# Probabilities times values in a forgetting-attention block: single key tiles against up to 512 query columns, nine full turned banks a head instead of ten partly filled ones

## The chip, the cores and the metric

The kernel runs on one core of one Trainium2 chip. The metric is the device time of one execution in microseconds (us). A core has five engines with instruction streams of their own: TensorE (PE, its weight loads shown apart as PEld), VectorE (DVE), ScalarE (ACT), GpSimd (POOL) and SyncE (SP, which here issues nearly all DMAs). Each stream runs in order, and the streams meet only where one instruction waits for another's semaphore.

## The reference, cut to what matters

The whole program is one decoder layer: RMSNorm, an input projection, forgetting attention beside chunked spatial gating, an output projection, and a convolutional gated MLP. The change lies in the attention alone. It has 1024 positions, 8 heads of 64, float32:

```python
logits = jnp.einsum('bqhd,bkhd->bhqk', qi, k).astype(jnp.float32) * scale
logits = logits + ci[..., None] - c_k                 # c: running sum of log-sigmoid forget gates
causal = pi[:, None] >= key_pos[None, :]
logits = jnp.where(causal, logits, -jnp.inf)
p = jax.nn.softmax(logits, axis=-1).astype(v.dtype)
return jnp.einsum('bhqk,bkhd->bqhd', p, v)
```

Queries are cut into 8 blocks of 128, here called rows j = 0 to 7, and keys into 8 tiles of 128, k = 0 to 7. The mask leaves the 36 blocks with k <= j.

## The kernel before, in words

**Number format.** TensorE works on float32r operands. To keep float32 accuracy a tensor is split into a rounded high part and the remainder, and products are summed over the parts. For the values, the high and the low part of V stand side by side as the 128 columns of one stationary operand, so one matmul gives both products, on partitions 0 to 63 and 64 to 127. The turned probabilities are split into high and low part too (s = 0, 1), so each product of a key tile with some query columns is two matmuls.

**A head, step by step.** The loop from line 1051 runs over 40 steps, five a head (s = 0 to 4), and works on two heads at once: the values of head h and the logits of head h+1. The order of TensorE's instructions is pinned by `seq`, which ties each to the one before. In each step TensorE gets, in this order:

1. the turns for the *next* step (`turn_p`, L946): blocks of probabilities, 128x128, are transposed into a PSUM bank. ScalarE casts the bank to the high part in a tile `pt` (L947), and VectorE subtracts to get the low part (L948). The tile pool gives `pt` three buffers.
2. for each group of this step: its value matmuls (`values`, L965), then the logits of the rows that `NEXT[s]` names (`logits_mm`, L906 and L907): rows 7, 6, then 5 and 4, then 3 and 2, then 1 and 0 in steps 0 to 4. VectorE takes from each row of logits the masked minimum of the negated logits (L919, `logits_min`).
3. in some steps (`FILLS`: steps 1 and 4 of heads 0 to 5, and three more of head 0's and the prologue's) a filler of 12 matmuls of the spatial gating's output projection (L990 to L992) with a VectorE add (L993).

The exponentials of the rows whose logits were made in a step are put on ScalarE at the end of the *next* step (`for e in last`, L1086 to L1088), behind that step's casts and, where there is one, behind its evacuation copy `out_copy` (L973). So rows 5 and 4 of head h+1 get their logits in step 2 and their exponentials (L929) in step 3; rows 3 and 2 in step 4; rows 1 and 0 in step 0 of the next head. In the last two heads the lists `held` and `last` shift this by a step.

**How the value product is tiled.** Queries go in pairs of rows: i = 3 is rows 6 and 7, i = 0 is rows 0 and 1. A group (h, i, k0) holds the two key tiles k0 and k0+1 against the 256 query columns of pair i: four blocks, or three where k0 = 2i lies on the diagonal. A head has ten groups: (3,0) (3,2) | (3,4) (3,6) | (2,0) (2,2) | (2,4) (1,0) | (1,2) (0,0), with | between steps. Six of their banks are 512 columns wide and four 384. Two PSUM banks a head, `po`, collect the result: rows 4 to 7, and rows 0 to 3. Each is evacuated by ScalarE and VectorE (L973, L974) into `attF`.

**Memory that is shared.** Four PSUM banks of tag `b` serve the turns, `po`, the filler and the turned row sums (`row_tail`, L868); two pairs of banks, tag `L`, serve the logits, so the logits of a row wait for the minimum of the row two before.

Of the kernel before, what the change touches and what calls it, by code (L numbers as in the profile page):

```python
# [12 lines left out]
ALU = mybir.AluOpType  # L13
AX = mybir.AxisListType
P = 128
# [44 lines left out]
def after(tc, later, earlier):  # L60
    tc.add_manual_dep(later.ins, earlier.ins.name, mybir.DependencyInfo(
        mybir.DependencyClass.NoSync, mybir.DependencyReason.DATA), reason="order")
# [3 lines left out]
def block_kernel(ctx: ExitStack, tc: tile.TileContext, xT, xtok, wuv, wv0, wv1, wqk, cpk, bfv,  # L66
                 ggain, g2r, gfr, wsp, woa, wos, wup, wdn, out):
    nc = tc.nc
    act, dve, pool, pe, sp = Line(nc.scalar, tc), Line(nc.vector, tc), Line(nc.gpsimd, tc), nc.tensor, nc.sync
# [13 lines left out]
    def nm(s):  # L83
        uid[0] += 1
        return f"{s}_{uid[0]}"
# [6 lines left out]
    def sb(tag, shape, dt=F32):  # L92
        return (raws if tag == "raw" else late if tag in LATE else early).tile(shape, dt, tag=tag, bufs=BUFS[tag], name=nm(tag))

    def bank():
        return psa.tile([P, 512], F32, tag="b", bufs=BB, name=nm("pb"))
# [7 lines left out]
    def f32(ap):  # L104
        return ap.bitcast(F32)
# [19 lines left out]
    ident = cst.tile([P, P], F32, name="ident")  # L125
# [77 lines left out]
    def psq(tag):  # L203
        return psa.tile([P, 512], F32, tag="s" if tag in "ab" else "b", bufs=4, name=nm("q" + tag))
# [12 lines left out]
    tj = sb("G", [P, 2, 2, 512])  # L217
# [478 lines left out]
    def seq(m):  # L696

        if order:
            after(tc, m, order[0])
        order[:] = [m]  # L700
# [106 lines left out]
    abs_, places = [None] * 8, {}  # L807
# [50 lines left out]
    attF = [None] * 4  # L858
# [15 lines left out]
    def pair_half(p, o):  # L874

        if attT[p] is None:
            attT[p] = sb("A" if p < 2 else "G", [P, 2, 1024], F32R)
        f, t = attF[p], attT[p]
        if p < 3:
            pool.tensor_tensor(out=f[:, 0, o], in0=f[:, 0, o], in1=f[:, 1, o], op=ALU.mult)  # L880
            pool.tensor_copy(t[:, 0, o], f[:, 0, o])
            pool.tensor_tensor(out=t[:, 1, o], in0=f[:, 0, o], in1=f32(t[:, 0, o]), op=ALU.subtract)
        else:
            dve.tensor_tensor(out=f[:, 0, o], in0=f[:, 0, o], in1=f[:, 1, o], op=ALU.mult)
            act.copy(t[:, 0, o], f[:, 0, o])
            dve.tensor_tensor(out=t[:, 1, o], in0=f[:, 0, o], in1=f32(t[:, 0, o]), op=ALU.subtract)
# [5 lines left out]
    def place():  # L892
        return psa.tile([P, 1024], F32, tag="L", bufs=2, name=nm("pl"))
# [4 lines left out]
    casts, los = [], []  # L898

    def logits_mm(h, j, ps):  # L900
        A, B, A2, B2 = abs_[h][:, 0, :], abs_[h][:, 1, :], a2s[0:66, h % 2, :], b2s[0:66, h % 2, :]
        n = (j + 1) * P
        qs = slice(j * P, (j + 1) * P)
        for c in range(0, n, 512):
            e = min(n, c + 512)
            seq(pe.matmul(ps[:, c:e], A[:, qs], B[:, c:e], start=True, stop=False))  # L906
            seq(pe.matmul(ps[:, c:e], A2[:, qs], B2[:, c:e], start=False, stop=True))  # L907
        return ps

    def logits_min(h, j, ps):  # L910

        i, jj = j // 2, j % 2
        w1, w2 = (2 * i + 1) * P, (2 * i + 2) * P
        if jj == 1:
            tp = sb(TTAG[i][h % 2], [P, w1 + w2])
            places[h, i] = (tp[:, 0:w1], tp[:, w1:w1 + w2])
        n = (j + 1) * P
        mn = sml.tile([P, 1], F32, tag="mn", name=nm("mn"))
        m = dve.tensor_tensor_reduce(out=places[h, i][jj], in0=ps[:, 0:n], in1=msk[:, 1024 - n:1024], scale=1.0,  # L919
                                     scalar=lim[:, 0:1], op0=ALU.add, op1=ALU.min, accum_out=mn)  # L920
        if h and j == 6:
            after(tc, m, recips[h - 1])
        if h and j == 3:
            after(tc, m, los[-1])
        return mn

    def logits_exp(h, j, mn):
        t = places[h, j // 2][j % 2]
        exs.append(act.activation(t, t, AF.Exp, bias=mn, scale=-1.0, accum_out=rows[h][:, j:j + 1]))  # L929
        return exs[-1]  # L930

    def logits(h, j):
        logits_exp(h, j, logits_min(h, j, logits_mm(h, j, place())))

    def turn_p(g):

        h, i, k0 = g
        tj = places[h, i]
        ptr = bank()
        pt = sb("pt", [P, 2, 512], F32R)  # L940
        diag = k0 == 2 * i
        blocks = [(k0, 0, 0), (k0, 1, 128)] + ([(k0 + 1, 1, 256)] if diag else
                                              [(k0 + 1, 0, 256), (k0 + 1, 1, 384)])
        w = 384 if diag else 512
        for k, jj, c in blocks:
            seq(pe.transpose(ptr[:, c:c + P], tj[jj][:, k * P:(k + 1) * P], ident))  # L946
        casts.append(act.copy(pt[:, 0, 0:w], ptr[:, 0:w]))  # L947
        los.append(dve.tensor_tensor(out=pt[:, 1, 0:w], in0=ptr[:, 0:w], in1=f32(pt[:, 0, 0:w]), op=ALU.subtract))  # L948
        return pt

    po = [None]

    def values(g, pt):
        h, i, k0 = g
        if i % 2 == 1 and k0 == 0:
            po[0] = bank()
        oc = (i % 2) * 256
        for s in range(2):
            for k in (k0, k0 + 1):
                lhs = V[k // 2][:, k % 2, h, :, :].rearrange("p s d -> p (s d)")  # L960
                half = k == 2 * i + 1
                o = (k - k0) * 256
                n = 128 if half else 256
                oo = oc + (128 if half else 0)
                seq(pe.matmul(po[0][:, oo:oo + n], lhs, pt[:, s, o:o + n], start=(k == 0 and s == 0),  # L965
                              stop=(s == 1 and half)))
        if i % 2 == 0 and k0 == 2 * i:
            p, hh = h // 2, h % 2
            o = slice((i // 2) * 512, (i // 2) * 512 + 512)
            r = slice(hh * 64, hh * 64 + 64)  # L970
            if attF[p] is None:
                attF[p] = sb("H", [P, 2, 1024])
            x = act.copy(attF[p][r, 0, o], po[0][64:128, :])  # L973
            dve.tensor_tensor(out=attF[p][r, 0, o], in0=po[0][0:64, :], in1=attF[p][r, 0, o], op=ALU.add)  # L974
            return x
        return None

    def sg_out(whs):
        for hf in range(2):
# [35 lines left out]
                pool.tensor_tensor(out=w[hf][:, 1], in0=src, in1=f32(w[hf][:, 0]), op=ALU.subtract)  # L1015
            wo.append(w)

    STEPS = [[(h, i, 2 * c) for i in (3, 2, 1, 0) for c in range(i + 1)] for h in range(8)]
    STEPS = [s[n:n + 2] for s in STEPS for n in range(0, 10, 2)]

    NEXT = (((7,), ()), ((6,), ()), ((5,), (4,)), ((3,), (2,)), ((1,), (0,)))

    def fill(key):
        for _ in range(FILL.get(key, 0)):
# [21 lines left out]
    for j in range(4, -1, -1):  # L1046
        logits(0, j)
        fill((-1, j))
    due = []
    turned = [turn_p(g) for g in STEPS[0]]  # L1050
    for n, step in enumerate(STEPS):
        h, s = n // 5, n % 5
# [7 lines left out]
        if h in (2, 4, 6) and s == 4:  # L1060
            for o in (slice(0, 512), slice(512, 1024)):
                pair_half(h // 2 - 1, o)
        now, turned = turned, [turn_p(g) for g in STEPS[n + 1]] if n + 1 < len(STEPS) else []
        last, due = due, []
        if n == 34:
# [10 lines left out]
        out_copy = None  # L1076
        for c, (g, pt, js) in enumerate(zip(step, now, NEXT[s])):
            out_copy = values(g, pt) or out_copy
            last_copy = out_copy
            if h < 7:  # L1080
                for j in js:
                    due.append((h + 1, j, logits_min(h + 1, j, logits_mm(h + 1, j, place()))))
            if s == (1 if h < 7 else 2) and c == (h == 7):
                row_tail(h)

        for e in last:  # L1086
            x = logits_exp(*e)
# [192 lines left out]
    for i in range(AHEAD):  # L1280
        for j in range(2):
            q = psq("a")
# [396 lines left out]
```

## Time and profile before

| | |
|---|---|
| median of 3 runs | 1058.69 us (1058.6 to 1058.9) |
| the profiled execution | 1059.72 us, its span 1058.0 us |
| instructions in the span | 14612 |
| TensorE busy | 1046.3 us, 99% of the span |
| VectorE, ScalarE, GpSimd busy | 884.0, 571.1, 235.8 us |
| first and last value matmul (L965) | 231.5 us, 370.0 us |

Rows of the profile give the engine, the line of the kernel, the operation, what it writes and reads, the shape, a count, and a duration; in the timeline the first column is the start in us from the span's start and the second the length of the run of like instructions. A matmul's length in a row includes its way through the array; the spacing of starts is what it costs in a stream. Where a row ends in brackets, they hold the idle time before it and what ended it. PEclk is the TensorE clock that was granted, in tenths of full speed.

### The profile page before, as it was taken

How to read it: one execution, taken by the hardware profiler on the slowest of the kernel's cores; microseconds unless marked ns; L12 is line 12 of the kernel's file. 1: busy time of each engine (PE TensorE's matmuls, PEld its weight loads, DVE VectorE, ACT ScalarE, POOL GpSimd, SP SyncE). 2: the span in 40 equal slices, each digit the busy share in tenths (PEclk: the TensorE clock that was granted, in tenths of full speed). 3: DMA queues.
4: the chain of work that ended last, by engine and by line, in shares of the span. 5: the costliest groups of instructions: out<-in, count | busy, mean ns of one | idle time of the engine just before them, and what ended most of it. 6: DMA issues, size and time to landing. Idle time of an engine off the chain costs nothing.

```text
span 1058.0 us, 14612 instructions
## 1 busy us (share of the span) xinstructions
PE 1046.3 (99%) x5156; PEld 880.3 (83%) x5156; DVE 884.0 (84%) x1297; ACT 571.1 (54%) x1013; POOL 235.8 (22%) x177
## 2 busy tenths in 40 slices
PE   9999999999999999999999999999999999999997
PEld 6988888988889888888888888888888888888885
DVE  6999787777778869998999989989897866897774
ACT  6776544456766746654444444444444544454653
POOL 0003241420420740154333323323321000000000
PEclk9999999999999999999999999999999999999999
DMA  9623466856555344222255322331322899333432
GB/s 323 219 8 134 129 162 167 224 153 190 168 163 170 122 174 173 72 89 100 80 170 179 120 96 94 120 122 59 132 96 80 302 328 314 102 99 100 146 119 94
DMA packets 67184, 155.78 MB, mean 147 GB/s; under 512 B 9028, under 2 KB 9748, under 8 KB 67112
## 3 DMA queue, kind: packets, MB, share of 16 engines
q1 hardware_dynamic: 65800, 154.82, 45.8%
q8 instruction: 40, 0.66, 0.3%
q14 instruction: 32, 0.26, 0.1%
q10 hardware_dynamic: 1312, 0.04, 0.1%
HBM read 111.96 MB, written 42.87 MB: 146 GB/s over the span
## 4 chain that ended last, share of the span: by engine, by line
PE 94%; DVE 2%; DMA 1%; ACT 1%; POOL 1%; issue 0%; SPq 0%; POOLq 0%; ACTq 0%; DVEq 0%
PE k L1529 20%; PE qc L1271 11%; PE qa L1271 11%; PE qd L1271 11%; PE ps L259 5%; PE qb L1271 5%; PE pb L259 5%; PE pb L965 3%; PE pb L946 3%; PE qa L417 2%; PE qc L417 2%; PE qd L417 2%; PE pl L906 2%; PE pl L907 2%; PE pf L990 1%; PE pf L992 1%
## 5 line engine op out<-in xcount | busy, mean ns | idle before, releaser
L1529 PE MATMUL k<-whb,wha 128*128 128x512 f32 x924 | 209.7, 389 | 0.0
L1529 PEld LDWEIGHTS k<-whb,wha 128*128 128x128 f32 x924 | 173.4, 188 | 36.2 <-DVE wha L161 0.2
L1271 PE MATMUL qc<-xT,whb 128*128 128x512 f32 x540 | 129.8, 389 | 0.2 <-ACT whb L155 0.2
L1271 PE MATMUL qa<-xB,wha 128*128 128x512 f32 x528 | 127.5, 390 | 0.0
L1271 PEld LDWEIGHTS qc<-xT,whb 128*128 128x128 f32 x540 | 101.3, 188 | 21.5 <-ACT whb L155 0.5
L1271 PEld LDWEIGHTS qa<-xB,wha 128*128 128x128 f32 x528 | 98.8, 188 | 20.9 <-DVE wha L161 0.4
L155 ACT CAST wha<-sg 128x512 fp32r<-128x512 f32 x77 | 47.8, 622 | 96.7 <-PE k L1529 86.4
L155 ACT CAST whb<-sg 128x512 fp32r<-128x512 f32 x82 | 50.5, 618 | 88.0 <-PE qc L1271 67.7
L161 DVE TENSOR_TENSOR wha<-sg,wha 128x512 fp32r<-128x512 f32 x77 | 52.7, 687 | 40.5 <-ACT wha L155 40.4
L947 ACT CAST pt<-pb 128x512 fp32r<-128x512 f32 (+1 forms) x80 | 42.2, 544 | 43.1 <-PE pb L946 34.2
L1271 PE MATMUL qd<-xB,whb 128*128 128x512 f32 x264 | 63.7, 389 | 0.0
L1271 PE MATMUL qd<-xT,whb 128*128 128x512 f32 x264 | 63.7, 389 | 0.0
L1155 POOL TENSOR_TENSOR sg<-raw 128x512 f32<-128x512 f32 x20 | 31.1, 1556 | 139.5 <-DVE whb L161 78.0
L1271 PE MATMUL qb<-xT,whb 128*128 128x512 f32 x252 | 61.0, 389 | 0.0
L161 DVE TENSOR_TENSOR whb<-sg,whb 128x512 fp32r<-128x512 f32 x82 | 57.0, 697 | 4.4 <-ACT whb L155 4.3
L948 DVE TENSOR_TENSOR pt<-pb,pt 128x512 fp32r<-128x512 f32 (+1 forms) x80 | 48.8, 634 | 12.3 <-ACT pt L947 11.0
L1271 PEld LDWEIGHTS qd<-xT,whb 128*128 128x128 f32 x264 | 49.5, 188 | 10.5 <-DVE u L1378 0.3
L1271 PEld LDWEIGHTS qd<-xB,whb 128*128 128x128 f32 x264 | 49.6, 188 | 10.3
L1271 PEld LDWEIGHTS qb<-xT,whb 128*128 128x128 f32 x252 | 47.2, 188 | 10.0 <-DVE whb L161 0.3
L965 PE MATMUL pb<-pt,V 128*128 128x256 f32 x320 | 52.1, 287 | 0.3 <-DVE pt L948 0.2
L1158 POOL TENSOR_TENSOR sg<-sg,raw 128x512 f32<-128x512 f32 x20 | 33.0, 1650 | 63.8 <-DVE whb L161 63.8
L965 PEld LDWEIGHTS pb<-pt,V 128*128 128x128 f32 x320 | 43.8, 190 | 2.6 <-DVE pt L948 0.4
(411 smaller groups left out, 2271.8 us busy)
## 6 DMA issues: line engine op xcount, KB each, us to landing
raw<-wup SPq DMA_DIRECT2D x44, 512.0 KB
sg<-hx SPq DMA_DIRECT2D x77, 256.0 KB
hx<-hs SPq DMA_DIRECT2D x44, 256.0 KB
hx<-ca SPq DMA_DIRECT2D x35, 256.0 KB
xT<-wdn SPq DMA_DIRECT2D x28, 256.0 KB
x<-kd SPq DMA_DIRECT2D x24, 256.0 KB
A<-xtok SPq DMA_DIRECT2D x8, 512.0 KB
raw<-wqk SPq DMA_DIRECT2D x8, 512.0 KB
```

Source lines behind the costliest of these rows:

```text
L155: act.copy(h, src)
L161: return eng.tensor_tensor(out=l, in0=src, in1=f32(h), op=ALU.subtract)
L259: pe.matmul(banks[m], xs(n, xi, k)[:, ms], w[:, wi, :], start=(first and k == 0 and c == 0 and (own or m % 2 == 0)), stop=(k == 3 and c == ...
L417: pe.matmul(ps, w[:, wi, ks], xs(n, xi, k), start=(first and c == 0), stop=(c == 11), skip_group_check=True)
L946: seq(pe.transpose(ptr[:, c:c + P], tj[jj][:, k * P:(k + 1) * P], ident))
L947: casts.append(act.copy(pt[:, 0, 0:w], ptr[:, 0:w]))
L948: los.append(dve.tensor_tensor(out=pt[:, 1, 0:w], in0=ptr[:, 0:w], in1=f32(pt[:, 0, 0:w]), op=ALU.subtract))
L965: seq(pe.matmul(po[0][:, oo:oo + n], lhs, pt[:, s, o:o + n], start=(k == 0 and s == 0), stop=(s == 1 and half)))
L1155: pool.tensor_tensor(out=s[0], in0=a21, in1=a22, op=ALU.add)
L1158: pool.tensor_tensor(out=s[3], in0=s[1], in1=a12, op=ALU.add)
L1271: pe.matmul(ps, w[:, wi, ks], xb[:, xi, k, :], start=(first and n == 0), stop=(n == 11), skip_group_check=True)
L1529: pe.matmul(banks[bk + m], xh[:, xi, ms], wh[:, wi, :], start=(first and p_ == 0 and n == 0), stop=(p_ == NP - 1 and n == 2), skip_group_c ...
```

## The change

The value product is cut the other way: one key tile k against all rows of a half that it reaches. Half 1 is rows 4 to 7, half 0 rows 0 to 3. A part (half, k) covers rows max(k, 4 half) to the end of the half, up to 512 columns. Parts are packed into nine groups of exactly four blocks: (1,0) to (1,4) alone, then (1,5) with (1,7), (1,6) with (0,2), (0,0) alone, and (0,1) with (0,3). The groups go two to a step, one in step 4, so the fifth entry of `NEXT` puts the logits of rows 1 and 0 behind that one group. The 36 turned blocks a head and the columns of the product are the same; the value matmuls are 24 a head instead of 40. Casts and subtractions are nine of 512 columns instead of six of 512 and four of 384. Both matmuls of one part now follow each other (s inside, k outside). The group (1,6)+(0,2) ends the first `po` bank and begins the second.

```diff
+    GROUPS = [((1, k),) for k in range(5)] + [((1, 5), (1, 7)), ((1, 6), (0, 2)), ((0, 0),), ((0, 1), (0, 3))]
+
+    def spans(g):
+
+        h, parts = g
+        c = 0
+        for half, k in parts:
+            j = max(k, 4 * half)
+            w = (4 * half + 4 - j) * P
+            yield half, k, j, c, w
+            c += w
+
     def turn_p(g):
 
-        h, i, k0 = g
-        tj = places[h, i]
         ptr = bank()
         pt = sb("pt", [P, 2, 512], F32R)
-        diag = k0 == 2 * i
-        blocks = [(k0, 0, 0), (k0, 1, 128)] + ([(k0 + 1, 1, 256)] if diag else
-                                              [(k0 + 1, 0, 256), (k0 + 1, 1, 384)])
-        w = 384 if diag else 512
-        for k, jj, c in blocks:
-            seq(pe.transpose(ptr[:, c:c + P], tj[jj][:, k * P:(k + 1) * P], ident))
-        casts.append(act.copy(pt[:, 0, 0:w], ptr[:, 0:w]))
-        los.append(dve.tensor_tensor(out=pt[:, 1, 0:w], in0=ptr[:, 0:w], in1=f32(pt[:, 0, 0:w]), op=ALU.subtract))
+        for half, k, j0, c, w in spans(g):
+            for j in range(j0, 4 * half + 4):
+                o = c + (j - j0) * P
+                seq(pe.transpose(ptr[:, o:o + P], places[g[0], j // 2][j % 2][:, k * P:(k + 1) * P], ident))
+        casts.append(act.copy(pt[:, 0, :], ptr))
+        los.append(dve.tensor_tensor(out=pt[:, 1, :], in0=ptr, in1=f32(pt[:, 0, :]), op=ALU.subtract))
         return pt
 
-    po = [None]
+    po = [None, None]
 
     def values(g, pt):
-        h, i, k0 = g
-        if i % 2 == 1 and k0 == 0:
-            po[0] = bank()
-        oc = (i % 2) * 256
-        for s in range(2):
-            for k in (k0, k0 + 1):
+        h, x = g[0], None
+        for half, k, j, c, w in spans(g):
+            new = (half, k) in ((1, 0), (0, 2))
+            if new:
+                po[half] = bank()
+            o = (j - 4 * half) * P
+            for s in range(2):
                 lhs = V[k // 2][:, k % 2, h, :, :].rearrange("p s d -> p (s d)")
-                half = k == 2 * i + 1
-                o = (k - k0) * 256
-                n = 128 if half else 256
-                oo = oc + (128 if half else 0)
-                seq(pe.matmul(po[0][:, oo:oo + n], lhs, pt[:, s, o:o + n], start=(k == 0 and s == 0),
-                              stop=(s == 1 and half)))
+                seq(pe.matmul(po[half][:, o:o + w], lhs, pt[:, s, c:c + w], start=(new and s == 0),
+                              stop=(s == 1 and (half, k) in ((1, 6), (0, 3))), skip_group_check=True))
...
-    STEPS = [[(h, i, 2 * c) for i in (3, 2, 1, 0) for c in range(i + 1)] for h in range(8)]
-    STEPS = [s[n:n + 2] for s in STEPS for n in range(0, 10, 2)]
-
-    NEXT = (((7,), ()), ((6,), ()), ((5,), (4,)), ((3,), (2,)), ((1,), (0,)))
+    STEPS = [[(h, g) for g in GROUPS[n:n + 2]] for h in range(8) for n in range(0, 9, 2)]
+
+    NEXT = (((7,), ()), ((6,), ()), ((5,), (4,)), ((3,), (2,)), ((1, 0),))
```

The evacuation copies keep their form and stand behind the parts (1,6) and (0,3).

More of the change, by code (lines that the diff above doesn't have):

```diff
@@ L949, in turn_p @@
+        casts.append(act.copy(pt[:, 0, :], ptr))
+        los.append(dve.tensor_tensor(out=pt[:, 1, :], in0=ptr, in1=f32(pt[:, 0, :]), op=ALU.subtract))
         return pt
-    po = [None]
+    po = [None, None]
     def values(g, pt):
-        h, i, k0 = g
-        if i % 2 == 1 and k0 == 0:
-            po[0] = bank()
-        oc = (i % 2) * 256
-        for s in range(2):
-            for k in (k0, k0 + 1):
-                lhs = V[k // 2][:, k % 2, h, :, :].rearrange("p s d -> p (s d)")
-                half = k == 2 * i + 1
-                o = (k - k0) * 256
-                n = 128 if half else 256
-                oo = oc + (128 if half else 0)
-                seq(pe.matmul(po[0][:, oo:oo + n], lhs, pt[:, s, o:o + n], start=(k == 0 and s == 0),
-                              stop=(s == 1 and half)))
[L967 to L976, printed above, removed]
@@ new lines, in values @@
+        h, x = g[0], None
[5 more added lines that the diff above has]
+            for s in range(2):
+                lhs = V[k // 2][:, k % 2, h, :, :].rearrange("p s d -> p (s d)")
+                seq(pe.matmul(po[half][:, o:o + w], lhs, pt[:, s, c:c + w], start=(new and s == 0),
+                              stop=(s == 1 and (half, k) in ((1, 6), (0, 3))), skip_group_check=True))
+            if (half, k) in ((1, 6), (0, 3)):
+                p, hh = h // 2, h % 2
+                q = slice(half * 512, half * 512 + 512)
+                r = slice(hh * 64, hh * 64 + 64)
+                if attF[p] is None:
+                    attF[p] = sb("H", [P, 2, 1024])
+                x = act.copy(attF[p][r, 0, q], po[half][64:128, :])
+                dve.tensor_tensor(out=attF[p][r, 0, q], in0=po[half][0:64, :], in1=attF[p][r, 0, q], op=ALU.add)
@@ L978, in sg_out @@
+        return x
     def sg_out(whs):
```

## The prediction

> **What bounds the kernel now.** I read the page first, then busy time by stretches, then one turn of a head on TensorE (PE) and ScalarE (ACT).
>
> ```profile
> span 1058.0 us, 14612 instructions
> PE 1046.3 (99%) x5156; PEld 880.3 (83%) x5156; DVE 884.0 (84%) x1297; ACT 571.1 (54%) x1013; POOL 235.8 (22%) x177
> ...
> PEclk9999999999999999999999999999999999999999
> ...
> L947 ACT CAST pt<-pb 128x512 fp32r<-128x512 f32 (+1 forms) x80 | 42.2, 544 | 43.1 <-PE pb L946 34.2
> ```
> ```profile
> 286.00:305.00 19.00, 19.00 (x129) 17.15 (x128) 14.85 (x32) 12.90 (x31) 0.27 (x1) 1.00 0.52 153
> ```
>
> PE is busy 99% of the span at the full granted clock, and in a stretch of 19 us, about one head, for all of it (second number), with DVE at 14.85 and ACT at 12.90. So time that PE gains or loses in the attention is time of the kernel, and ACT has slack as long as PE never asks for something that ACT does late. The next two answers show where ACT is late: PE, then ACT, from step 3 of head 2 (rows of head 3 in `H`) to the filler of step 4.
>
> ```profile
> 282.73 0.52 PE L946 MATMUL pb<-ident,wy 128*128 128x128 f32 x3
> 283.09 0.49 PE L946 MATMUL pb<-ident,gg 128*128 128x128 f32 x3
> 283.33 0.65 PE L965 MATMUL pb<-pt,V 128*128 128x256 f32 x4
> 283.82 0.45 PE L906 MATMUL pl<-x 128*128 128x512 f32 x1
> 284.11 0.39 PE L907 MATMUL pl<-x,x 66*128 66x512 f32 x1
> 284.34 0.63 PE L965 MATMUL pb<-pt,V 128*128 128x256 f32 x4
> 284.81 0.34 PE L906 MATMUL pl<-x 128*128 128x384 f32 x1
> 284.99 0.34 PE L907 MATMUL pl<-x,x 66*128 66x384 f32 x1
> 285.16 1.04 PE L946 MATMUL pb<-ident,H 128*128 128x128 f32 x8
> 285.96 0.65 PE L965 MATMUL pb<-pt,V 128*128 128x256 f32 x4
> 286.54 0.39 PE L906 MATMUL pl<-x 128*128 128x256 f32 x1
> 286.77 0.28 PE L907 MATMUL pl<-x,x 66*128 66x256 f32 x1
> 286.89 0.58 PE L965 MATMUL pb<-pt,V 128*128 128x256 f32 x4
> 287.30 0.27 PE L906 MATMUL pl<-x 128*128 128x128 f32 x1
> 287.41 0.28 PE L907 MATMUL pl<-x,x 66*128 66x128 f32 x1
> 287.53 0.45 PE L990 MATMUL pf<-whl,G 128*128 128x512 f32 x1
> ```
> ```profile
> 283.29 0.48 ACT L947 CAST pt<-pb 128x384 fp32r<-128x384 f32 x1 [0.56 <-PE pb L946]
> 284.02 0.48 ACT L947 CAST pt<-pb 128x384 fp32r<-128x384 f32 x1 [0.26 <-PE pb L965]
> 284.52 0.58 ACT L973 COPY H<-pb 64x512 f32<-64x512 f32 x1
> 285.01 0.94 ACT L929 ACTIVATE H<-H,mn 128x768 f32<-128x768 f32 x1
> 285.85 0.19 ACT L929 ACTIVATION_READ_ACCUMULATOR H<-H,mn 128x1 f32 x1
> 285.94 0.82 ACT L929 ACTIVATE H<-H,mn 128x640 f32<-128x640 f32 x1
> 286.66 0.19 ACT L929 ACTIVATION_READ_ACCUMULATOR H<-H,mn 128x1 f32 x1
> ```
>
> What to see: at 285.16 PE turns the first banks of the next head, while ACT is only at that head's rows 5 (768 keys, from 285.01) and 4 (640 keys, done at 286.66 + 0.19 = 286.85). Before the change this is harmless, because groups (3,0) and (3,2) hold rows 6 and 7 alone, whose exponentials ran in steps 1 and 2.
>
> **The change part by part.**
>
> *The new wait.* The first two groups are now (1,0) and (1,1): rows 4 to 7. Their turns are issued at the same place, and the loop over j begins with row 4, so the first turn of step 4 waits for the exponential that is last in step 3. In the built order it carries a wait on ACT for just that instruction. PE's order is pinned, so everything behind stands still: eight turns, the values of step 4, the logits of rows 1 and 0, the filler.
>
> How late is it? Step 3 is counted from its first turn. On PE, step 3 has four turns instead of six. Six took 283.33 − 282.73 = 0.60, eight took 285.96 − 285.16 = 0.80, so a turn costs 0.10 and four 0.40. Group (1,6)+(0,2) is four matmuls of 256. Four of 256 took 284.81 − 284.34 = 0.47, 0.12 each; the first four, two of them of 128, took 283.82 − 283.33 = 0.49 behind the turns, so four of 256 there are 0.61. Logits of row 3: 0.52. Group (0,0) is two of 512: 0.23 each (284.11 to 284.34), 0.46. Logits of row 2: 0.35. PE reaches the turn after 0.40 + 0.61 + 0.52 + 0.46 + 0.35 = 2.34 us (before: 2.43).
>
> On ACT: the first cast began 0.56 after the first turn, with three turns in its bank; with four it begins at 0.66. It is 512 wide: from the 544 ns mean of 48 such and 32 of 0.48, it takes 0.59. There is no second cast: step 4 has one group. So the copy L973 begins at 1.27 (its values end earlier, near 0.9), against 284.52 − 282.73 = 1.79 before. From this copy's start to row 4's end took 286.85 − 284.52 = 2.33. The other parity of heads:
>
> ```profile
> 303.35 0.58 ACT L973 COPY H<-pb 64x512 f32<-64x512 f32 x1
> ...
> 305.61 0.19 ACT L929 ACTIVATION_READ_ACCUMULATOR t<-t,mn 128x1 f32 x1
> ```
>
> There it is 305.80 − 303.35 = 2.45. So row 4 is ready at 3.60 or 3.72; its minimum holds nothing up, it was there 284.15 − 282.73 = 1.42 after the first turn:
>
> ```profile
> 284.07 0.08 DVE L919 DVE_READ_ACCUMULATOR2_ANT mn<- 128x1 f32 x1
> ```
>
> The exponential cannot start before 2.6. With 0.05 until PE starts (an estimate), PE stands still 1.31 or 1.43 us. Seven heads' logits are made in the loop, four of the first parity: 4 × 1.31 + 3 × 1.43 = 9.5 us. Lower bound, if the wait ends with the exponential itself, not with its accumulator read, and at once: 0.14 less each, 8.5. Upper bound, with another 0.1 to restart: 10.2.
>
> *What the wait covers.* The values of step 4 took 286.54 − 285.96 = 0.58 where the like in step 3 took 0.49, and 287.30 − 286.89 = 0.41 where 2 × 0.12 + 2 × 0.06 = 0.36 is their own: the logits of rows 1 and 0 waited there for minima. PE comes later now, and these 0.14 us go, seven times: −1.0 (0 to −1.3).
>
> *The value matmuls.* Before: 32 of 256 and 8 of 128 a head. After: 12 of 512, 4 of 384 and 256 each, 4 of 128. By the rows 0.23, 0.18 (284.81 to 284.99), 0.12, and for 128 half of 0.12 (an estimate; at most 0.085, from the 0.41 above): 4.32 becomes 2.76 + 0.72 + 0.48 + 0.24 = 4.20 a head. That is 0.12, over eight heads −1.0 (with 0.085: −1.8). A matmul here costs by its columns, and these stay the same; 16 fewer instructions bring almost nothing.
>
> The Trainium skill speaks for more: "TensorE: Matmul & The Clock Gate", section "Back-to-back issue gap", gives for streams of weight load and matmul about 81 ns at 128 columns and 131 at 512, a price mostly per instruction. Interpolated (an estimate from that page) the product would fall from 3.8 to 2.7 us a head, −8.2 in all, and the sum below would be about 0. The trace disagrees: 230 ns at 512 and 120 at 256, nearly twice.
>
> *Off the path.* Turns are 36 a head as before, casts and subtractions 1.07 us for two in PE's shade; a cast no longer waits for values to give up a `pt` buffer in steps 3 and 4 (the 0.26 at 284.02). In steps 0 to 2 each bank has the step's length from turn to use, as before. The filler of heads 0 to 5 behind step 4 (12 × 0.23 = 2.8 us) lets ACT and DVE catch up. No DMA and no POOL instruction moves past another; their loads come later by what PE loses.
>
> *The last head.* It has no logits of its own to fill PE, and waits already:
>
> ```profile
> 365.62 0.66 PE L946 MATMUL pb<-ident,wy 128*128 128x128 f32 x4 [0.49 <-DVE pt L948]
> ...
> 370.09 0.44 PE L1178 MATMUL pb<-whl,A 128*128 128x512 f32 x1
> ```
>
> There group (0,0) is turned in step 2 and now needs row 0, whose exponential was put into step 1, so this wait grows by up to 1 us; but the last step saves a cast and its wait, and part of head 6's standstill overlaps waits that stand here anyway. I take −0.2, between −0.5 and +1.0.
>
> *Sum.* 9.5 − 1.0 − 1.0 − 0.2 = +7.3 us on the profiled 1059.72 (span 1058.0 and 1.72 around it): 1067.0. The median of the runs is 1.03 lower, so the forecast for it is 1058.69 + 7.3 = **1066.0 us**. The bounds add to 8.5 − 1.8 − 1.3 − 0.5 = +4.9 and 10.2 − 1.0 − 0 + 1.0 = +10.2: 1063.6 to 1068.9.
>
> **The rivals.** A measurement of this kernel can tell about 0.2%, 2.1 us, from no change.
>
> - *The wait is covered.* Row 4 might be ready when PE gets there, if ACT began step 3 earlier by 1.3 us. Against: the first cast follows the turns of its own step, so ACT cannot start earlier than PE lets it. It would leave the values' −1.0 to −1.8: 1057.3, the same.
> - *A price per instruction, so faster.* Behind a turn a first value matmul pays more: 0.49 for four where 0.36 is their own. If each matmul paid such a fixed price p, 128 fewer would bring 128 p. From p above (9.5 − 1.0 − 0.2) / 128 = 0.065 us this outweighs the wait. At the full 0.13 it is −16.6: 1058.7 + 8.3 − 16.6 = 1050.4. Against: 0.47 for four of 256 and 0.23 for one of 512 leave a p near 0.005. This is the way in which the Trainium skill's rule above would decide.
> - *The clock falls.* If each standstill cost PE its full clock until the filler, the 287.53 − 285.16 = 2.37 us of step 4 would take twice as long: 7 × 2.37 = 16.6 more, 1082.6. Against: the clock row stays at 9 throughout.
>
> **How the numbers follow.** The standstill rests on a wait in the program and on durations seen seven times: 0.91. Covered 0.04, price per instruction 0.03, clock 0.02. The range takes the bounds of the sum and half a microsecond on each side for what one profiled execution leaves open: 1063.1 to 1069.4. Slower by over 0.2% then 0.93 (0.91 and the clock), within 0.2% 0.04, faster 0.03.
>
> **What would show each step.** In the profile after, the first turn of step 4 should have an idle PE of 1.2 to 1.5 us before it, ended by ACT L929, seven times, 9 to 10 us in all; it is the only new large wait. Value matmuls of 512 should start 0.23 apart, and the spacing of the few of 256 stay 0.12. The gap before the logits of rows 1 and 0 should go. If idle time before these turns is under 0.5 us, or 512-wide ones start under 0.2 apart, I am wrong; if the standstill is there and the time is not up by 5 us or more, something behind it had slack that I took for none.

## The result, and the profile after

| | before | after |
|---|---|---|
| median on the same chip | 1058.86 us (6 runs, 1058.6 to 1059.05) | 1066.09 us (6 runs, 1065.82 to 1066.97) |
| ratio, 95% interval | | 1.0069 [1.0059, 1.008] |
| profiled execution, its span | 1059.72, 1058.0 us | 1065.97, 1064.2 us |

The changed kernel is slower by 7.2 us; 1066.0 was forecast. The page of after, in the lines that answer to those of before:

```profile
span 1064.2 us, 14345 instructions
PE 1044.6 (98%) x5028; PEld 872.1 (82%) x5028; DVE 883.8 (83%) x1289; ACT 571.5 (54%) x1005; POOL 236.2 (22%) x177
...
PEclk9999999999999999999999999999999999999999
```

PE did a little less work (1044.6 us busy instead of 1046.3, 128 matmuls fewer) in a longer span, at the same clock: the time went into standing still. Where, the waits of after on PE in the attention say (engine, line, what it waited for: us in total, times, longest):

```profile
PE pb L954 <- ACT H L929: 5.0, 4, 1.3
PE pb L954 <- ACT t L929: 4.1, 3, 1.4
PE pb L954 <- ACT gg L929: 0.7, 1, 0.7
PE pb L970 <- DVE pt L956: 0.3, 1, 0.3
```

Seven waits of a turn on an exponential, 9.1 us, four where the rows lie in `H` and three where they lie in `t`: the new wait, at the place and with the parity that the prediction named. The 0.7 is the last head's. The stretch that the prediction walked through, in the timeline of after (head 2's step 3 from its first turn to the logits of row 1; first PE, then ACT):

```profile
283.83 0.30 PE L954 MATMUL pb<-ident,gg 128*128 128x128 f32 x1
283.97 0.49 PE L954 MATMUL pb<-ident,wy 128*128 128x128 f32 x3
284.21 0.72 PE L970 MATMUL pb<-pt,V 128*128 128x256 f32 x4
284.77 0.39 PE L906 MATMUL pl<-x 128*128 128x512 f32 x1
285.00 0.40 PE L907 MATMUL pl<-x,x 66*128 66x512 f32 x1
285.24 0.64 PE L970 MATMUL pb<-pt,V 128*128 128x512 f32 x2
285.72 0.34 PE L906 MATMUL pl<-x 128*128 128x384 f32 x1
285.90 0.33 PE L907 MATMUL pl<-x,x 66*128 66x384 f32 x1
287.49 1.09 PE L954 MATMUL pb<-ident,H 128*128 128x128 f32 x8 [1.25 <-ACT H L929]
288.33 0.77 PE L970 MATMUL pb<-pt,V 128*128 128x384 f32 x4
288.94 0.33 PE L906 MATMUL pl<-x 128*128 128x256 f32 x1
```
```profile
284.50 0.59 ACT L955 CAST pt<-pb 128x512 fp32r<-128x512 f32 x1 [0.76 <-PE pb L954]
285.11 0.59 ACT L978 COPY H<-pb 64x512 f32<-64x512 f32 x1
285.59 0.94 ACT L929 ACTIVATE H<-H,mn 128x768 f32<-128x768 f32 x1
286.43 0.19 ACT L929 ACTIVATION_READ_ACCUMULATOR H<-H,mn 128x1 f32 x1
286.52 0.82 ACT L929 ACTIVATE H<-H,mn 128x640 f32<-128x640 f32 x1
287.24 0.19 ACT L929 ACTIVATION_READ_ACCUMULATOR H<-H,mn 128x1 f32 x1
```

Row 4 is ready at 287.24 + 0.19 = 287.43, 3.60 after the first turn; PE goes on at 287.49. The bracket gives 1.25 idle, but it counts from the end of the last matmul, 0.33 after its start. In a stream the next one would have started 0.18 after it, so PE was ready at 285.90 + 0.18 = 286.08, 2.25 after the first turn, and lost 1.41.

The times from each PE instruction's start to the next one's, summed by what the instruction does, from the first value matmul to the first instruction behind the last, give the account of the attention (us, one profiled execution each):

| | before | after | difference |
|---|---|---|---|
| logits, with the standstill behind them | 32.01 | 42.19 | +10.18 |
| value matmuls | 41.11 | 39.11 | −2.00 |
| turns | 29.08 | 28.79 | −0.29 |
| filler | 36.39 | 36.14 | −0.25 |
| whole stretch | 138.59 | 146.23 | +7.64 |

Behind the stretch both take 687.9 us more. Ahead of it the profiled execution of after was 1.4 us shorter (its first value matmul at 230.13, before's at 231.49), though the change touches nothing there; over the eleven profiled executions told of here that start lies anywhere between 230.1 and 231.5. So the two spans differ by 6.2 only, while the medians differ by 7.2 and the attention itself by 7.6.

### The profile page after: what moved, and what is told of

Its sections match the earlier page's. It is cut to its first block, busy times and chain, and to the rows that moved or that the text cites. A ratio compares the mean times of both kernels' runs of the same rounds, so it can differ in the third digit from the quotient of the medians.

```text
span 1064.2 us, 14345 instructions
## 1 busy us (share of the span) xinstructions
PE 1044.6 (98%) x5028; PEld 872.1 (82%) x5028; DVE 883.8 (83%) x1289; ACT 571.5 (54%) x1005; POOL 236.2 (22%) x177
## 4 chain that ended last, share of the span: by engine, by line
PE 94%; ACT 3%; DVE 2%; issue 1%; ACTq 0%
PE k L1532 20%; PE qc L1274 11%; PE qa L1274 11%; PE qd L1274 11%; PE ps L259 6%; PE pb L259 5%; PE qb L1274 5%; PE pb L954 3%; PE pb L970 2%; PE qa L417 2%; PE qc L417 2%; PE qd L417 2%; PE pf L994 1%; PE pf L995 1%; PE pf L996 1%; PE pl L906 1%
## 5 line engine op out<-in xcount | busy, mean ns | idle before, releaser
L955 ACT CAST pt<-pb 128x512 fp32r<-128x512 f32 x72 | 41.1, 588 | 51.1 <-PE pb L954 44.1
L956 DVE TENSOR_TENSOR pt<-pb,pt 128x512 fp32r<-128x512 f32 x72 | 48.6, 689 | 19.3 <-ACT pt L955 18.8
L970 PE MATMUL pb<-pt,V 128*128 128x512 f32 (+3 forms) x192 | 49.7, 363 | 0.4 <-DVE pt L956 0.3
L1161 POOL TENSOR_TENSOR sg<-sg,raw 128x512 f32<-128x512 f32 x20 | 33.3, 1665 | 63.4 <-DVE whb L161 63.4
L1159 POOL TENSOR_TENSOR sg<-sg,raw 128x512 f32<-128x512 f32 x20 | 35.2, 1758 | 47.2 <-issue 44.6
```

The costliest lines, as they stand in the source:

```text
L955: casts.append(act.copy(pt[:, 0, :], ptr))
L956: los.append(dve.tensor_tensor(out=pt[:, 1, :], in0=ptr, in1=f32(pt[:, 0, :]), op=ALU.subtract))
L970: seq(pe.matmul(po[half][:, o:o + w], lhs, pt[:, s, c:c + w], start=(new and s == 0), stop=(s == 1 and (half, k) in ((1, 6), (0, 3))), ski ...
L1159: pool.tensor_tensor(out=s[1], in0=s[0], in1=a11, op=ALU.add)
L1161: pool.tensor_tensor(out=s[3], in0=s[1], in1=a12, op=ALU.add)
```

## The experiments

**1. Part of the wait away.** After, with the turns of a bank issued from the last row down, so that row 4 is wanted last:

```diff
-            for j in range(j0, 4 * half + 4):
+            for j in reversed(range(j0, 4 * half + 4)):
```

> The changed kernel, with the rows of each turned part taken from the highest to the lowest. If PE stands still for row 4's exponential alone, the three turns of rows 7, 6 and 5 of the first bank of step 4 now lie inside the wait instead of behind it: three turns of 0.109 us, 0.33 us a head, seven heads: 2.3 us less than the changed kernel, 1063.8 us (1063.2 to 1064.4). PE's idle time before turns falls from 9.2 us to about 7 us. If the standstill were about something else at that place (a PSUM bank, the restart of PE, the first value matmul), the order of the rows would change nothing: 1066.1 us.

Measured: 1063.34 us, ratio to before 1.0042 [1.0026, 1.0059]; 2.75 us less than after, in the range expected. The idle time fell further than to the 7 us expected, to 5.3. Its waits, and the turns of head 2's step 4:

```profile
PE pb L954 <- ACT H L929: 2.8, 8, 0.5
PE pb L954 <- ACT t L929: 2.5, 6, 0.5
```
```profile
285.53 0.38 PE L954 MATMUL pb<-ident,H 128*128 128x128 f32 x2
286.13 0.33 PE L954 MATMUL pb<-ident,H 128*128 128x128 f32 x1 [0.22 <-ACT H L929]
286.94 0.77 PE L954 MATMUL pb<-ident,H 128*128 128x128 f32 x5 [0.48 <-ACT H L929]
```

The one wait of 1.25 became two: rows 7 and 6 are turned at once, then PE waits for row 5's exponential, then for row 4's. Three turns of the bank fill part of the standstill, and the time went down with it. In starts, logits and turns together take 68.35 us instead of 70.98, 2.63 less, and the whole stretch 143.55 instead of 146.23, 2.68 less: what the standstill loses, the kernel gains.

**2. The wait alone.** Before, with its pairs in the order 2, 3, 1, 0, so that its first turn too needs row 4. Its matmuls, widths and banks stay:

```diff
-        if i % 2 == 1 and k0 == 0:
+        if i in (2, 1) and k0 == 0:
...
-        if i % 2 == 0 and k0 == 2 * i:
+        if (i, k0) in ((3, 6), (0, 0)):
...
-    STEPS = [[(h, i, 2 * c) for i in (3, 2, 1, 0) for c in range(i + 1)] for h in range(8)]
+    STEPS = [[(h, i, 2 * c) for i in (2, 3, 1, 0) for c in range(i + 1)] for h in range(8)]
```

> The kernel before, with one thing changed: its pairs of rows go 2, 3, 1, 0 instead of 3, 2, 1, 0, so that the first two groups of a head need rows 5 and 4. No wide matmul, ten banks, 40 value matmuls. Theory: the wait alone makes the loss, and here it is longer, because step 3 still has two casts ahead of the copy: row 4 is ready 4.17 or 4.29 us after step 3's first turn and PE is there after 2.43, so 1.74 or 1.86 us seven times, 12.5, less the 1.0 that the logits of rows 1 and 0 no longer wait: 1070.4 us (1068.8 to 1071.5). If the loss of the change comes from the widening, this stays at 1058.9.

Measured: 1071.58 us, 1.0118 [1.0103, 1.0133]. Waits on PE, and the turns behind two of them, in head 1 and head 2:

```profile
PE pb L946 <- ACT t L929: 5.1, 3, 1.7
PE pb L946 <- ACT H L929: 5.0, 4, 1.6
PE pl L906 <- DVE mn L919: 1.5, 1, 1.5
```
```profile
269.22 1.52 PE L946 MATMUL pb<-ident,t 128*128 128x128 f32 x8 [1.70 <-ACT t L929]
291.34 1.09 PE L946 MATMUL pb<-ident,H 128*128 128x128 f32 x8 [1.58 <-ACT H L929]
```

The old tiling with the new wait loses 12.7 us, so the tiling itself is not what makes after slow. Forecast were 1068.8 to 1071.5, so it came out 0.1 above the range. Six of the waits came as expected: from the last logits to the turn they add 1.74 or 1.86 us. In head 6 a row's logits waited 1.5 for a minimum, which had not been counted, and the turn after it waited only 0.3.

In the profiled execution, which took 1072.61, something more happened. The granted clock was 0.5 from 269.73 to 273.14 us, right behind head 1's standstill, and eight turns took 1.52 there instead of 1.09. Head 1 took 22.3 us, heads 2 to 5 20.5 to 20.7, so the low clock cost some 1.7 us. The other standstills of the attention left the clock full, two of 1.69 and 1.70 among them; what set this one apart is not shown. Whether it happened in the other three runs (1070.09 to 1071.61) is not known.

**3. The wait away, by moving the turn.** After, with step 4's turns of the next head put behind its values and the filler, ahead of the logits of rows 1 and 0; the exponentials of step 3's logits are put on ScalarE ahead of them:

```diff
+        behind_fill = s == 4 and h < 7
-        now, turned = turned, [turn_p(g) for g in STEPS[n + 1]] if n + 1 < len(STEPS) else []
+        now, turned = turned, [turn_p(g) for g in STEPS[n + 1]] if n + 1 < len(STEPS) and not behind_fill else []
...
             out_copy = values(g, pt) or out_copy
+            if behind_fill:
+                for e in last:
+                    after(tc, logits_exp(*e), out_copy)
+                last = []
+                fill((h, s))
+                turned = [turn_p(g) for g in STEPS[n + 1]]
...
-        fill((h, s))
+        if not behind_fill:
+            fill((h, s))
```

> The changed kernel, with step 4's turns of the next head put behind step 4's values and its filler, ahead of the logits of rows 1 and 0. Same instructions, same wait. Theory: for heads 0 to 5 the 2.8 us filler covers the 1.4 us, so six standstills go and PE reaches the turns late; head 6 has no filler and keeps about 0.7. 1057.0 us (1056.0 to 1058.7), a little under the kernel before. If the added time lies in the wide matmuls or in full banks rather than in the wait, it stays at 1065 or above.

Measured: 1060.11 us, 1.001 [1.0001, 1.0019]. Six of the seven standstills are gone and 6.0 us with them, but not the 9 that were expected: new waits stand in their place.

```profile
PE pb L970 <- DVE pt L956: 1.6, 2, 1.3
PE pl L906 <- DVE mn L919: 1.2, 5, 0.2
PE pb L954 <- ACT H L929: 0.7, 1, 0.7
PE pb L954 <- ACT gg L929: 0.7, 1, 0.7
```

Row 7's logits in step 0 now follow so close on row 1's that they wait for its minimum to give up the bank, five times. The 1.3 is in head 1, where four casts of weights stood ahead of the turns' casts on ScalarE:

```profile
268.78 2.16 ACT L155 CAST whl<-raw 128x512 fp32r<-128x512 f32 x4
270.97 1.56 ACT L955 CAST pt<-pb 128x512 fp32r<-128x512 f32 x3
```

**4. The same with the turns last.** As 3, but in heads 0 to 5 the turns go behind the logits of rows 1 and 0:

```diff
                 fill((h, s))
-                turned = [turn_p(g) for g in STEPS[n + 1]]
+                if h == 6:
+                    turned = [turn_p(g) for g in STEPS[n + 1]]
             if h < 7:
...
+            if behind_fill and h < 6:
+                turned = [turn_p(g) for g in STEPS[n + 1]]
```

> The run e2_turn_behind_filler came out at 1060.11, above its 1056.0 to 1058.7: its PE waits 0.23 us six times ahead of row 7's logits for row 1's minimum, because the logits of rows 1 and 0 had moved behind the turns, and in spacing this is 0.49 each. Here step 4 of heads 0 to 5 goes values, filler, logits of rows 1 and 0, turns; head 6 stays as in that run. If that is the reason, six times 0.49 go: 1057.2 us (1056.3 to 1058.5). If not, it stays near 1060.

Measured: 1059.16 us, 1.0006 [0.9997, 1.0015], again above what was expected. The wait for minima is gone; the 1.3 behind the weight casts, the 0.7 of head 6 and the 0.7 of the last head are as in 3. New is what the timeline of PE shows behind the filler of head 2:

```profile
289.77 1.94 PE L954 MATMUL pb<-ident,H 128*128 128x128 f32 x16
291.85 0.74 PE L970 MATMUL pb<-pt,V 128*128 128x512 f32 x2
```

Two steps' turns now stand in a row, and the values of the first come right behind, before their bank is cast and subtracted: the 16 turns hold PE for 2.08 us. From the last turn to the first value matmul it is 0.42 us in five heads (in head 1 this is where the wait of 1.3 stands), where it is 0.03 elsewhere and in all but the first of after: 5 × 0.39 = 2.0. A turn put late loses its distance to its values.

**5. The wait away, by making the logits a step earlier.** After, with rows 7 and 6 in step 0, 5 and 4 in step 1, and so on, none in step 4 (the dependence of row 6's minimum on the reciprocals, which come in step 1, had to go):

```diff
-        if h and j == 6:
-            after(tc, m, recips[h - 1])
...
-    NEXT = (((7,), ()), ((6,), ()), ((5,), (4,)), ((3,), (2,)), ((1, 0),))
+    NEXT = (((7,), (6,)), ((5,), (4,)), ((3,), (2,)), ((1,), (0,)), ((), ()))
```

> The changed kernel, with the logits two rows a step from step 0 (7 and 6, 5 and 4, 3 and 2, 1 and 0, none in step 4), so that rows 5 and 4 have their exponentials in step 2; the condition that puts row 6's minimum behind the reciprocal of the row sums is left out, as it would point at a later step. Theory: no turn waits for an exponential, and the 9.2 us of idle PE go. ACT gets 3.3 us of casts and exponentials in step 2 and hands over the bank of step 4 late, which may cost 0.2 to 0.5 us a head before the values of step 4. 1058.2 us (1056.5 to 1060). If the loss is in the widening, 1065 or more.

Measured: 1058.5 us, 0.9997 [0.9988, 1.0006], 7.6 less than after. No wait on ScalarE is left in the attention; one on VectorE is new:

```profile
PE pb L952 <- DVE pt L954: 2.6, 7, 0.6
```

**6. The early logits with the narrow tiling.** The same two edits made in before.

> The kernel before (ten banks, 40 value matmuls of 256 and 128), with the same early logits as in the run e4_logits_early. Beside that run it shows what the new tiling is worth where neither waits for row 4. Theory: matmuls cost by their columns, so this is 1.0 to 1.8 us slower than e4_logits_early and no more. A price per instruction of 0.065 us or above would make it slower by 8 us or more.

Measured: 1059.44 us, 1.0007 [0.9998, 1.0015], 0.94 slower than 5, just below the range expected. The value matmuls take 40.62 us between starts against 39.29 in 5.

**7. The early logits with the wide tiling's matmuls cut in two.** As 5, but no matmul over 256 columns, so 320 of them as in before:

```diff
-                seq(pe.matmul(po[half][:, o:o + w], lhs, pt[:, s, c:c + w], start=(new and s == 0),
-                              ...
+                for d in range(0, w, 256):
+                    n = min(256, w - d)
+                    seq(pe.matmul(po[half][:, o + d:o + d + n], lhs, pt[:, s, c + d:c + d + n],
+                                  start=(new and s == 0 and d == 0),
+                                  ...
```

> e4_logits_early with one thing changed: each value matmul wider than 256 columns is cut into two (512 into 256 and 256, 384 into 256 and 128), 40 value matmuls a head again over the same nine banks in the same order. Theory: 12 cuts of 512 a head at 0.24 for 0.23 and four of 384 at 0.18 for 0.18: 0.1 us a head, 0.5 to 1.5 us slower than e4_logits_early in all. By a price per instruction of 0.065 us it would be 8 us slower.

Measured: 1058.03 us, 0.9994 [0.9985, 1.0003]: 0.47 less than 5 where 0.5 to 1.5 more was expected. That is a miss, and the cause is not in PE. The values do take longer, 41.70 us between starts instead of 39.29, but the turns take 28.87 instead of 31.55. On VectorE 5 and 7 turned out to differ: the scheduler had placed the subtraction L954 behind row 1's minimum in 5, ahead of it in 7. VectorE in 5, from the minimum of row 3 to that subtraction, and PE's turns that wait for it:

```profile
282.15 0.74 DVE L919 CUSTOM_DVE_ANT_0 wy<-pl,t,lim 128x512 f32<-128x512 f32 x1
...
283.61 0.48 DVE L919 CUSTOM_DVE_ANT_0 gg<-pl,t,lim 128x256 f32<-128x256 f32 x1 [0.17 <-PE pl L907]
284.02 0.08 DVE L919 DVE_READ_ACCUMULATOR2_ANT mn<- 128x1 f32 x1
284.02 0.69 DVE L954 TENSOR_TENSOR pt<-pb,pt 128x512 fp32r<-128x512 f32 x1
```
```profile
283.94 0.62 PE L952 MATMUL pb<-ident,H 128*128 128x128 f32 x4
284.85 0.63 PE L952 MATMUL pb<-ident,H 128*128 128x128 f32 x4 [0.28 <-DVE pt L954]
```

The second bank of step 4's turns is the one that this subtraction gives up; it ends at 284.71, 0.4 after PE was through with the first four turns. So 5 against 7 was no clean measurement of the width.

**8 and 9. The order on VectorE held, then the width alone.** 8 is 5 with row 1's minimum tied behind the last subtraction; 9 is 7 with the same. VectorE and ScalarE then have one order in both (9's is also the order that 7 had):

```diff
-        if h and j == 3:
+        if h and j in (3, 1):
             after(tc, m, los[-1])
```

> The logits-early kernel (wide value matmuls), with one dependence more: row 1's minimum on DVE stands behind the last low-part subtraction, as row 3's does already. In the logits-early run that minimum stood ahead of the subtraction and the next turn's bank came free late (2.6 us idle, seven times); in its split form the scheduler had, unasked, put the subtraction first, and the wait was 0.8, once. Theory A (the split form's 0.47 us came from that order of DVE, and a matmul has a small price of its own): the wait goes here too, the turns take some 28.9 instead of 31.55 us and the values stay at 39.3: 1058.5 - 2.6 = 1055.9, between 1055.4 and 1056.8. Theory B (more, narrower matmuls are no dearer or even cheaper, the order is nothing): 1058.5, the wait stays.

> The pinned kernel with its value matmuls cut to 256 columns or fewer, 128 more of them; DVE and ACT have the same order in both. Only the price of 128 instructions is left between the two. Theory A: the split values took 2.4 us more (41.70 against 39.29 between starts), 0.019 us for each, and here nothing absorbs it: 2.4 us slower than the pinned wide one, about 1058.1, between 1.2 and 2.6 slower. Theory B: no difference, within 0.4 us. A price of 0.065 us or more for each, from which the change as it stands would have been faster, would be 8.3 us or more.

Measured: 8 takes 1056.67 us, 0.9978 [0.9969, 0.9987]; 9 takes 1058.03 us, 0.9992 [0.9983, 1.0001], the same as 7. The waits of 8, and its PE and VectorE at the place shown of 5:

```profile
PE pb L952 <- DVE pt L954: 0.9, 1, 0.9
PE pl L906 <- DVE mn L919: 0.3, 1, 0.3
PE pb L968 <- DVE pt L954: 0.3, 1, 0.3
```
```profile
284.22 1.21 PE L952 MATMUL pb<-ident,H 128*128 128x128 f32 x8
285.19 0.76 PE L968 MATMUL pb<-pt,V 128*128 128x384 f32 x4
```
```profile
283.63 0.08 DVE L919 DVE_READ_ACCUMULATOR2_ANT mn<- 128x1 f32 x1
284.02 0.69 DVE L954 TENSOR_TENSOR pt<-pb,pt 128x512 fp32r<-128x512 f32 x1 [0.31 <-ACT pt L953]
...
285.24 0.47 DVE L919 CUSTOM_DVE_ANT_0 gg<-pl,t,lim 128x256 f32<-128x256 f32 x1
```

The seven waits are one. The gain is 1.8 us, not 2.6, though within the 1055.4 to 1056.8 expected: the eight turns still need 0.97 us here, where eight took 0.84 in after, so a part of the wait stays in the spacing. Against 9, which differs only in the width, 8 is 1.36 us faster by the medians, inside the 1.2 to 2.6 expected: 0.011 us for each of 128 matmuls. In starts, the values differ by 41.66 − 39.62 = 2.04 and the turns give 0.65 back. This is the value of the wider matmuls; it is there, and it is small. The whole tiling, nine full banks for ten as well, is worth up to 2.8 us (1059.44 − 1056.67, experiments 6 and 8), but VectorE's and ScalarE's orders differ between these two, so that figure is not clean. The Trainium skill's rule that the prediction weighed ("TensorE: Matmul & The Clock Gate", section "Back-to-back issue gap") would have made it 8.2 us, by the prediction's estimate from that page; the runs do not bear it out for this stream.

Kernel 8 is the best version here: the changed tiling, with the logits a step earlier and one order on VectorE held, is 2.2 us faster than before and 9.4 faster than the change as it was made.

## Why the prediction was right

- *The new wait* was the step that decided, and it held: seven waits of a turn on L929, four of 1.25 us and three of about 1.38. The idle time sums to 9.1, in the forecast's 9 to 10. In spacing the loss is 10.2, at the top of the step's 8.5 to 10.2 and 0.7 above the 9.5 taken. The reason is on PE: ACT's row 4 was ready 3.60 after the first turn as worked out, piece by piece (the cast began at 0.67, the copy at 1.28), and the 0.05 to restart was 0.06, but PE was there at 2.25 instead of 2.34, because the first values and row 3's logits took 0.05 less each. Experiments 1, 2, 3 and 5 show it as the cause: it goes down with the wait, comes with the wait alone, and goes with it.
- *The waits covered and the value matmuls* were to bring −1.0 each, and both sizes held. In before, the last value matmul ahead of row 1's logits took 0.155 to 0.286 to the next start, where 0.06 is its own: 1.07 over seven heads. In after row 3's minimum was there at 287.07, and these logits started at 288.94. But the prediction read its rows wrongly in part: row 0's logits did not wait in before (0.06 ahead of them in every head), and row 1's waited longer in the heads of the other parity (0.28), which made up for it. The rest of the values' gain is 1.2 in heads 0 to 6. Experiments 8 and 9 put the width at 1.4, in another order of work. Matmuls of 512 start 0.23 apart and those of 256 0.12, as the signs asked.
- *Off the path* held: turns and filler changed by 0.3 us each, the turns through the last two heads, and no wait but those named stands in the list of after with more than 0.3 us.
- *The last head* has its wait for row 0 (0.7 on `gg`), as the step had it, up to 1. Its net was taken as −0.2. The same account by heads has it: head 7, from its first value matmul to the first instruction behind its last, takes 0.54 more, and head 6's turns take 0.77 less, since two stops that PE has there in before are gone (in starts 0.45 between two banks' turns and 0.32 ahead of the values). Together this is −0.23.
- *The rivals.* The wait was not covered. The price per instruction is 0.011 us, a sixth of the 0.065 at which it would have outweighed the wait. The clock stayed full in after from 5 to 1060 us, so its standstills of 1.25 to 1.38 cost just their own length. But the rival is less far off than the prediction thought: experiment 2, with standstills of 1.58 to 1.70, shows a halved clock behind one of them.
- *The sum* of +7.3 stands against +7.2 between medians and +7.6 in the attention. It is that close in part by luck: the standstill was 0.7 larger in spacing, and against it the values of the first seven heads gave 0.4 more back than the two steps had for them, and the medians differ by 0.4 less than the attention.

The forecasts of the experiments did worse than that of the change. Those of 3 and 4 took the standstill away without asking what comes next at the turn's new place, and 7's took VectorE's order for unchanged. That of 2 had no term for the wait for a minimum or for the clock.

## What to carry to other kernels

When a product is retiled, write down for every operand the latest producer that its *first* instruction now needs, and compare that with the program's place for it: here 128 matmuls saved were worth 1.4 us, and one operand needed a step too early cost 10. Mend such a wait at the producer (logits a step earlier, 1058.5 us and then 1056.67) rather than by putting the consumer late, which opened waits behind it (1060.11 and 1059.16). And where a scheduler orders the engines, compare the order of the other engines before a small difference is put down to the edit.

## What the runs showed of the hardware

A matmul split in two costs little: 0.011 us more by the medians, 0.016 in starts (2.04 / 128). The idle time in brackets understates what a stall costs a pipelined engine, here 1.25 for a loss of 1.41, since the last matmul's row still shows it at work for 0.15 us after the next one could have started. The first value matmul behind a turn pays 0.08 more to the next start: 0.20 instead of 0.12 at 256 columns in before, 0.31 instead of 0.23 at 512 in after. There are 46 such places in either kernel's attention, so the price goes by the place, not by the matmul, and the change does not touch it. And a standstill can cost more than its length: in experiment 2's profile the granted clock was 0.5 for 3.41 us right behind one of 1.70, and full behind all seven of after, 1.25 to 1.38.
